# Row sums over a 64 MB stream: one load into the first buffer, with a 1 KB scratch read issued ahead of it

## The chip, the cores and the metric

The kernel runs on one core of a Trainium2 chip. The metric is the device time of one execution in microseconds (us). Some executions of a program can fall in a slower state; all runs of the two kernels, and of every variant that was timed in rounds (before and variant in turn), were in the fast state, with a granted clock of 1.0.

## The reference

```python
def setup_inputs():
    batch, seq, dim = 32, 512, 1024
    return {"x": np.random.randn(batch, seq, dim).astype(np.float32)}

def reference(x):
    return np.sum(x, axis=-1).astype(np.float32)
```

There are 16,384 rows of 1,024 float32, 67.11 MB in. 64 KB come out.

## The kernel before

The rows are cut into two blocks of 112 and 16 rows per partition. A buffer `xt` takes 16 rows on each of 128 partitions, which is 64 KB a partition and 8.39 MB in all, and there are three such buffers. DVE (VectorE) sums 16 rows with one reduction. ACT (ScalarE) helps only near the end. All loads are issued by SP (SyncE). The first buffer is filled by two loads: one row per partition, then the other 15.

```python
    xpool = ctx.enter_context(tc.tile_pool(name="x", bufs=3))
    ...
        while c < whole:
            m = min(G, whole - c)                       # G = 16
            xt = xpool.tile([P, G * D], F32, tag="xt", name="xt")
            parts = (0, 1, m) if done + c == 0 else (0, m)
            for i, k in zip(parts, parts[1:]):
                nc.sync.dma_start(
                    out=xt[:, i * D : k * D], in_=x_b[:, (c + i) * D : (c + k) * D]
                )
            a = ACT_ROWS if done + c + m == full else 0
            rows_dve(xt, res, 0, m - a, c)
            rows_act(xt, res, m - a, a, c + m - a)
            c += m
    ... # the last 16 rows of each partition in six smaller loads, summed by DVE and ACT
```

After the program is built, the first `EARLY = 2` DMA instructions of SP are moved from the body into the entry block, ahead of the barrier with which the engines start:

```python
    loads = [i for i in code if i.engine == sp][:EARLY]
    for load in loads:
        assert load.opcode == "DMACopy" and not load.sync_info.on_wait
        code.remove(load)
    ...
    at = next(k for k, i in enumerate(code) if i.engine == sp and i.opcode == "Drain")
    code[at:at] = loads
```

## Time and profile before

| What | Before | Where it is read |
|---|---|---|
| time | 162.29 us (162.26 to 162.44, 3 runs) | times |
| span of the profiled run | 160.5 us | page |
| one 16-row reduction on DVE | 17.22 us | groups by form |
| one 8.39 MB buffer | every 19.35 us, 433.5 GB/s | starts of the reductions in the timeline |
| first reduction starts | 21.81 us | timeline |

The first fence has two lines of the groups kept apart by form: line, engine, operation, names, shapes and count; then busy us and mean ns; then the idle time before the group and what ended it. The second is from the waits: who waited for whom, us in total, times, longest.

```profile
line engine op names shapes xcount | busy us, mean ns | idle before us <-releasers
L41 DVE TENSOR_REDUCE res<-xt 128x16 f32<-128x16384 f32 x6 | 103.3, 17220 | 32.4 <-DMA xt<-in_x_dram 32.4
```

```profile
DVE res L41 <- DMA xt<-in_x_dram: 34.5, 7, 21.8
```

DVE always waits for DMA: 21.8 us for the first buffer, and about 2.1 us for each of the others, since a buffer takes 19.35 us to arrive and 17.22 us to sum. The timeline shows the pace (start, duration, then the instruction):

```profile
21.81 17.22 DVE L41 TENSOR_REDUCE res<-xt 128x16 f32<-128x16384 f32 x1 [21.81 <-DMA xt<-in_x_dram]
41.09 17.22 DVE L41 TENSOR_REDUCE res<-xt 128x16 f32<-128x16384 f32 x1 [2.06 <-DMA xt<-in_x_dram]
60.44 17.22 DVE L41 TENSOR_REDUCE res<-xt 128x16 f32<-128x16384 f32 x1 [2.13 <-DMA xt<-in_x_dram]
...
118.49 17.22 DVE L41 TENSOR_REDUCE res<-xt 128x16 f32<-128x16384 f32 x1 [2.13 <-DMA xt<-in_x_dram]
```

The Trainium skill, "DMA: Bandwidth & Descriptors", section "Where 436 GB/s comes from", gives 435.2 GB/s as the ceiling of the 16 SBUF ports that the DMA engines write through; the 433.5 GB/s here agree within 0.4%. (The same section says that for loads from HBM a lower limit of about 358 GB/s binds, though it also names a load measured at 425; here the measured pace lies above both.) By this ceiling the kernel has next to nothing to gain from the first buffer on. What is left is the start.

The start is best seen in two views. First, SP's line of the timeline: its first four loads, of which the first, row 0, is issued at 0.00 us.

```profile
0.00 2.28 SPq L79 DMA_DIRECT2D xt<-in_x_dram  x4
```

Then the view of busy time by stretches: the stretch, its length, the busy time of DVE, ACT and POOL, the clock, the DMA share (mean of 16 engines), and GB/s.

```profile
0.00:1.00 1.00, 0.00 (x0) 0.00 (x0) 0.20 (x4) 1.00 0.00 0
1.00:1.50 0.50, 0.00 (x0) 0.00 (x0) 0.00 (x0) 1.00 1.42 115
1.50:2.00 0.50, 0.00 (x0) 0.00 (x0) 0.00 (x0) 1.00 0.39 147
2.00:2.50 0.50, 0.00 (x0) 0.00 (x0) 0.00 (x0) 1.00 1.00 401
```

A packet is one contiguous piece that a DMA engine moves. This view books a packet, with all its bytes and all its time, in the stretch in which it begins; that is why a share can exceed 1. It also lets one count packets and find their mean duration. From 1.0 to 1.5 us, 115 GB/s for 0.5 us are 57 KB, so 14 packets of 4 KB began. Their time is 1.42 x 0.5 us x 16 engines = 11.4 us, so 0.81 us each. From 2.0 to 2.5 us there are 49 packets of 4 KB with 1.00 x 8 = 8 us, so 0.16 us each. **The first packet on an engine is slow, by about 0.6 us; those behind it are not.** The stored trace also has the start, duration and size of every single packet, though not its engine, and `prof` has no view that lists them. The text calls these the packet records; engines are told apart in them only by which packet begins as another ends.

### The profile page before, as it was taken

To read this page: it belongs to the slowest core of one execution; us is meant where nothing else is said; L and a number is where in the kernel's file an instruction comes from. 1 tells how busy PE (TensorE), PEld (TensorE's weight loads), DVE (VectorE), ACT (ScalarE), POOL (GpSimd) and SP (SyncE) were. 2 spreads that over 40 slices of the span, in tenths; PEclk is the share of its full clock that TensorE was granted. 3 is DMA by queue.
4 is the path that set the end of the run, shared out by engine and by line. 5 is a ranking of instruction groups with operands and counts; after the bars stand their busy time and mean duration, and the time that the engine had idled before them with its cause. 6 is when DMAs were issued, how large, how long until landed. Compare 5 with 4: busy or idle time off the path is not lost.

```text
span 160.5 us, 118 instructions
## 1 busy us (share of the span) xinstructions
DVE 122.7 (76%) x14; ACT 16.0 (10%) x29; POOL 0.2 (0%) x4
## 2 busy tenths in 40 slices
DVE  0000059997799959999499994999949998699992
ACT  0000000000000000000000000000000000692892
POOL 0000000000000000000000000000000000000000
DMA  9979996996996996996996996996997998999991
GB/s 376 490 306 429 490 523 261 523 523 261 523 523 261 523 523 261 523 523 261 523 523 261 523 506 278 523 506 278 523 474 310 523 425 359 392 425 425 419 401 46
DMA packets 2304, 67.18 MB, mean 418 GB/s; under 512 B 512, under 2 KB 640, under 8 KB 1024
## 3 DMA queue, kind: packets, MB, share of 16 engines
q1 hardware_dynamic: 2160, 67.12, 97.3%
q10 hardware_dynamic: 144, 0.06, 0.1%
HBM read 67.11 MB, written 0.07 MB: 418 GB/s over the span
## 4 chain that ended last, share of the span: by engine, by line
DMA 74%; DVE 22%; SPq 1%; issue 0%; DVEq 0%
DMA xt<-in_x_dram 74%; DVE res L41 21%; SPq L93 1%; DVE xt L57 1%; DVEq L57 0%; DVE part L57 0%; DVEq L114 0%
## 5 line engine op out<-in xcount | busy, mean ns | idle before, releaser
L41 DVE TENSOR_REDUCE res<-xt 128x16 f32<-128x16384 f32 (+4 forms) x10 | 121.8, 12203 | 34.5 <-DMA xt<-in_x_dram 34.5
L49 ACT ACT_TABLE_LOAD x1 | 1.3, 1283 | 137.9 <-DMA xt<-in_x_dram 137.9
L49 ACT ACTIVATE xt<-xt 128x1024 f32<-128x1024 f32 x14 | 14.6, 1042 | 3.7 <-DVE res L41 3.7
L49 ACT ACTIVATION_READ_ACCUMULATOR xt<-xt 128x1 f32 x14 | 2.6, 186 | 0.0
L57 DVE CUSTOM_DVE_ANT_0 xt<-xt 128x288 f32<-128x288 f32 x1 | 0.5, 459 | 0.9 <-DMA xt<-in_x_dram 0.9
L57 DVE CUSTOM_DVE_ANT_0 xt<-xt,part 128x224 f32<-128x224 f32 x1 | 0.5, 452 | 0.1
L151 POOL MEMSET const-uint8-127<- 128x1 uint8 x1 | 0.1, 102 | 0.0
L151 POOL MEMSET const-bfloat16-1.0<- 128x1 bf16 x1 | 0.1, 101 | 0.0
L151 POOL MEMSET const-float32-0.0<- 128x1 f32 x1 | 0.1, 98 | 0.2 <-issue 0.2
L151 POOL MEMSET const-float32-1.0<- 128x1 f32 x1 | 0.1, 98 | 0.0
L57 DVE DVE_READ_ACCUMULATOR2_ANT res<- 128x1 f32 x1 | 0.1, 84 | 0.0
L57 DVE DVE_READ_ACCUMULATOR2_ANT part<- 128x1 f32 x1 | 0.1, 83 | 0.0
## 6 DMA issues: line engine op xcount, KB each, us to landing
xt<-in_x_dram SPq DMA_DIRECT2D x1, 7680.0 KB, 21.3
xt<-in_x_dram SPq DMA_DIRECT2D x1, 4096.0 KB, 31.1
xt<-in_x_dram SPq DMA_DIRECT2D x1, 2048.0 KB, 35.7
xt<-in_x_dram SPq DMA_DIRECT2D x2, 512.0 KB, 21.1
xt<-in_x_dram SPq DMA_DIRECT2D x1, 1024.0 KB, 37.8
xt<-in_x_dram SPq DMA_DIRECT2D x1, 288.0 KB, 38.9
xt<-in_x_dram SPq DMA_DIRECT2D x1, 224.0 KB, 38.9
xt<-in_x_dram SPq DMA_DIRECT2D x6, 40.8
```

Source lines behind the costliest of these rows:

```text
L41: nc.vector.tensor_reduce(out=res[:, c : c + n], in_=xt[:, j * D : (j + n) * D].rearrange("p (j d) -> p j d", d=D), axis=X, op=ADD,)
L49: nc.scalar.activation(out=v, in_=v, func=COPY, accum_out=acc)
L57: nc.vector.tensor_tensor_reduce(out=xt[:, a:h], in0=xt[:, a:h], in1=xt[:, h:b], scale=1.0, scalar=first, op0=ADD, op1=ADD, accum_out=acc,)
L93: nc.sync.dma_start(out=xt[:, i * D : k * D], in_=x_b[:, (c + i) * D : (c + k) * D])
L151: nc = _bacc.Bacc("TRN2", target_bir_lowering=False, num_devices=1)
```

## The change

Its intent, as the name `warm` says: let a tiny read meet that slow first access, so that the first buffer can come in one load without the split. The scratch tile is never read.

```diff
+    warm = rpool.tile([16, 16], F32, name="warm")
...
-            parts = (0, 1, m) if done + c == 0 else (0, m)
-            for i, k in zip(parts, parts[1:]):
-                nc.sync.dma_start(
-                    out=xt[:, i * D : k * D], in_=x_b[:, (c + i) * D : (c + k) * D]
-                )
+            if done + c == 0:
+                nc.sync.dma_start(out=warm, in_=x_flat[0:16, 0:16])
+            nc.sync.dma_start(out=xt[:, 0 : m * D], in_=x_b[:, c * D : (c + m) * D])
```

The rest of the diff changes no instruction. `EARLY` is still 2, so the scratch read and the whole first load now stand ahead of the barrier.

More of the change, by code (lines that the diff above doesn't have):

```diff
@@ L118 @@
     sp = mybir.EngineType.SP
+    fn = tc.nc.m.functions[0]
     entry, body = None, None
-    for blk in tc.nc.m.functions[0].blocks:
+    for blk in fn.blocks:
         ops = [i for i in blk.instructions if i.engine == sp]
```

## The prediction

> **What bounds the kernel.** The input stream. In the timeline the 16-row reductions on DVE start at 21.81, 41.09, ..., 118.49 and 137.84 us, so one 8.39 MB buffer arrives every 19.35 us ((137.84 - 41.09) / 5), which is 433.5 GB/s. The Trainium skill (DMA: Bandwidth & Descriptors, "Where 436 GB/s comes from") puts the ceiling at 435.2 GB/s; the trace agrees within 0.4%. One reduction takes 17.22 us (groups by form), so DVE waits some 2.1 us for each buffer, always on DMA (waits: 34.5 us in 7 waits, 21.8 of them the first load). The queue never runs dry: the load issues (DMA queue's waits) come when a reduction frees a buffer, e.g. at 39.06 us, while a whole further load is still queued. So the end is: start of the stream + 67.11 MB at 433.5 GB/s (154.8 us) + a tail. The last load lands at 157.1; 157.1 - 154.8 = 2.3 us is all that the start costs, and the change touches only this.
>
> **The start before, from the packet records.** Row 0's load is issued at 0.00 us, the load of rows 1 to 15 at 0.43, the next two at 1.26 and 1.64. First packets start at 1.00 us. They take 0.60 to 1.01 us on 14 of the 16 DMA engines, where later 4 KB packets take 0.159; on the other two the first packet starts only at 1.81 us. So every engine is slow once, [...]and ends its first packet 1.75 to 2.18 us in. Then come seven 4 KB packets (about 0.157 us each) and eight of 60 KB (2.27): 19.26 us per engine. The first buffer is full at 21.39 us.
>
> **What the change does.** Instruction order: two DMAs are still moved ahead of the start barrier, now the 1 KB scratch read and the whole first load; the other 14 DMAs, their order, the buffers and all compute are the same. One extra wait on a semaphore in the issue of the tail loads asks for something long done. Nobody reads the scratch tile.
> Removed: 128 packets of 4 KB. Added: 16 packets of 64 B. The first load becomes eight 64 KB packets per engine, at 2.418 us 19.34 us.
> If the slow first access is paid once per engine by whatever comes first, the scratch read pays it between 1.0 and about 1.65 to 2.05 us (estimate: row 0's first packet less its 0.16 us of transfer plus a little), and the big load, issued at 0.43 and ready about 1.0 us later (the same lag as row 0's), follows without a gap: full at about 21.3 us, 0.1 us earlier. If the big load has to pay a second latency behind it, it is 0.4 to 0.6 us later. If the 64 B return sooner than 0.6 us, up to 0.3 us earlier. Any of these passes one to one to the end.
>
> **Predicted.** 162.3 us, range 161.8 to 162.8; faster by over 2% 0.005, within 2% 0.985, slower by over 2% 0.01. A 2% change (3.2 us) is more than the whole 2.3 us of start.
>
> **What would show it.** Reductions still 19.35 us apart and 17.22 us long; the first begins at 21.7 us (21.4 to 22.3), and the end shifts by as much as it does. First big packets start at 1.5 to 2.1 us and take about 2.42 us, not 3. Span 160.1 to 161.0.
>
> **What would make it wrong.** A scratch read far slower than row 0's first packets (its 16 rows lie within 64 KB of memory, so all engines may press on one place); a big load whose descriptors come later than row 0's; or a first-packet penalty that depends on size or address, so that it is paid by each of the big load's partitions.

## The result

| | before | changed |
|---|---|---|
| time, median | 162.37 us (162.26 to 162.58, 4 runs) | 162.83 us (162.75 to 162.92, 4 runs) |
| span of the profiled run | 160.5 us | 161.0 us |
| first reduction starts | 21.81 us | 22.20 us |

The ratio is 1.0027, 95% interval [1.001, 1.0044]: 0.46 us slower, small but outside noise. (Ratios here are the mean time of one kernel's fast runs over that of the other's of the same rounds, so not quite the ratio of the medians.)

The timeline after, the same reductions:

```profile
22.20 17.22 DVE L42 TENSOR_REDUCE res<-xt 128x16 f32<-128x16384 f32 x1 [22.20 <-DMA xt<-in_x_dram]
41.55 17.22 DVE L42 TENSOR_REDUCE res<-xt 128x16 f32<-128x16384 f32 x1 [2.13 <-DMA xt<-in_x_dram]
60.90 17.22 DVE L42 TENSOR_REDUCE res<-xt 128x16 f32<-128x16384 f32 x1 [2.13 <-DMA xt<-in_x_dram]
...
118.96 17.22 DVE L42 TENSOR_REDUCE res<-xt 128x16 f32<-128x16384 f32 x1 [2.13 <-DMA xt<-in_x_dram]
```

Every start is 0.39 to 0.47 us later than before, from the first to the last. From the second reduction on the pace is the same 19.35 us. So 0.39 us of the loss is there by 22.2 us, and it is carried to the end. The other 0.07 comes between the first two reductions, which were 19.28 us apart before and are 19.35 now; why was not traced. The waits say the same: 35.0 us in place of 34.5, the longest 22.2 in place of 21.8.

```profile
DVE res L42 <- DMA xt<-in_x_dram: 35.0, 7, 22.2
```

The SP issues after, from the timeline, and the scratch read's line of the DMA issues (KB each, us from issue to landing):

```profile
0.00 0.38 SPq L79 DMA_DIRECT2D warm<-in_x_dram  x1
0.44 1.62 SPq L80 DMA_DIRECT2D xt<-in_x_dram  x3
```

```profile
warm<-in_x_dram SPq DMA_DIRECT2D x1, 1.0 KB, 1.5
```

The big load is issued at 0.44 us, where row 0 was issued at 0.00. The scratch read has landed by 1.5 us. Then the stretches after:

```profile
1.00:1.50 0.50, 0.00 (x0) 0.00 (x0) 0.00 (x0) 1.00 1.61 526
1.50:2.00 0.50, 0.00 (x0) 0.00 (x0) 0.00 (x0) 1.00 4.65 1573
...
4.50:5.00 0.50, 0.00 (x0) 0.00 (x0) 0.00 (x0) 1.00 4.54 1966
```

From 1.5 to 2.0 us 12 packets of 64 KB begin (1573 GB/s x 0.5 us = 786 KB), with 4.65 x 8 = 37.2 us: 3.10 us each. From 4.5 to 5.0 us, the second packet on each engine, there are 15 with 36.3 us: 2.42 us each. **The big load pays the slow first packet in full (0.68 us), although the scratch read has been through every engine just before.** In the packet records the 16 scratch packets begin at 0.99 to 1.18 us and last 8 ns each. Their landings, 16 of them, come from 1.30 to 1.45 us, so 8 ns is not the whole way of the data; but no scratch packet is recorded as slow, as row 0's first packets were.

### The profile page after: what moved, and what is told of

Read it like the earlier page. It is cut to its first block, busy times and chain, and to the rows that moved or that the text cites. A ratio compares the mean times of both kernels' runs of the same rounds, so it can differ in the third digit from the quotient of the medians.

```text
span 161.0 us, 117 instructions
## 1 busy us (share of the span) xinstructions
DVE 122.7 (76%) x14; ACT 16.1 (10%) x29; POOL 0.2 (0%) x4
## 4 chain that ended last, share of the span: by engine, by line
DMA 74%; DVE 22%; SPq 1%; issue 0%; DVEq 0%
DMA xt<-in_x_dram 74%; DVE res L42 21%; SPq L92 1%; DVE xt L58 1%; DVEq L58 0%; DVE part L58 0%; DVEq L113 0%
```

## The experiments

Theory A: the scratch read absorbs nothing. It takes the first issue slot of SP, about 0.43 us, and the bulk load behind it starts that much later and pays its slow first packet anyway. The rivals are told in the expectations. Eleven kernels were run, all with right results. Two of them (one buffer; the bursts) were slow on purpose, and had one look each, so their state is not known; only packet times within the one run are compared there.

Those timed in rounds are summed up in this table, worked out from the issues, packet records and reductions of the profiled runs; times are medians. "First packets" are the first 16 in time of the first load with a whole buffer or most of it (in the two rows with *, of row 0's load): first and last start, and mean duration. With packets as short as 4 KB a few of these 16 are an engine's second. A 64 KB packet takes 2.42 us later on, one of 63 KB (quarter row) 2.38.

```
kernel        bulk load   first packets     mean    first       minus    time    ratio to before
              issued, us  start, us         us      reduction   issue    us      [95%]
before         0.00*       1.00 to 1.80*    0.73*    21.81      21.81    162.33
no_warm        0.00        0.99 to 1.86     3.07     21.85      21.85    162.46  1.0002 [0.9990, 1.0015]
swapped        0.00        1.00 to 1.48     3.17     21.99      21.99    162.52  1.0006 [0.9994, 1.0019]
warm_act       0.00        1.00 to 1.56     3.14     21.74      21.74    162.37  0.9998 [0.9984, 1.0012]
changed        0.44        1.47 to 1.76     3.12     22.20      21.76    162.83  1.0027 [1.0010, 1.0044]
same_addr      0.43        1.47 to 2.38     2.99     22.19      21.76    162.96  1.0036 [1.0020, 1.0051]
warm4k         0.43        1.49 to 2.33     3.10     22.37      21.95    162.96  1.0035 [1.0022, 1.0049]
row0_warm      0.44*       1.47 to 1.75*    0.47*    22.53      22.09    162.87  1.0028 [1.0015, 1.0042]
late_load      0.79        1.76 to 2.26     3.19     22.64      21.85    163.12  1.0044 [1.0028, 1.0059]
two_warms      0.88        1.92 to 2.66     3.07     22.80      21.92    163.38  1.0062 [1.0049, 1.0075]
quarter_row    0.41**      1.48 to 2.53     3.02     22.43      22.02    162.68  1.0017 [1.0005, 1.0030]
* row 0's load, packets of 4 KB, later ones 0.159 us    ** the second load
```

The ratio is to the kernel before of the same rounds, whose median was 162.37 us for the changed kernel, 162.45 for warm_act and quarter_row, and 162.33 for the others.

The column to look at is "minus issue". Whatever stands ahead of the bulk load, the first reduction starts 21.7 to 22.1 us after that load is issued.

**no_warm: without the scratch read** (and with `EARLY = 1`, so that the later loads stay where they were).

```diff
-            if done + c == 0:
-                nc.sync.dma_start(out=warm, in_=x_flat[0:16, 0:16])
```

> The change without its scratch read: one load of 8 MB fills the first buffer and is the first DMA issued. Theory A (the scratch read absorbs nothing; it only takes the first issue slot of about 0.43 us, and the load behind it still pays the slow first packet): first big packets start at about 1.0 us instead of 1.47 to 1.76, take 2.9 to 3.4 us, first reduction at about 21.8 us, time equal to the kernel before within 0.1 us, about 0.4 us under the changed kernel. Rival B (a 64 KB first packet is dearer than a 4 KB one, so the split of row 0 was what helped): time stays 0.3 to 0.5 us above the kernel before.

Measured: 162.46 us (162.35 to 162.48, 5 runs), ratio 1.0002. The first reduction starts at 21.85 us:

```profile
21.85 17.22 DVE L42 TENSOR_REDUCE res<-xt 128x16 f32<-128x16384 f32 x1 [21.85 <-DMA xt<-in_x_dram]
```

As theory A says. One load of 8 MB is as good a start as row 0 and the rest, within the interval (-0.1% to +0.15%); rival B falls. The medians differ by 0.13 us, which these rounds don't resolve.

**swapped: the same two DMAs in the other order.**

```diff
-            if done + c == 0:
-                nc.sync.dma_start(out=warm, in_=x_flat[0:16, 0:16])
             nc.sync.dma_start(out=xt[:, 0 : m * D], in_=x_b[:, c * D : (c + m) * D])
+            if done + c == 0:
+                nc.sync.dma_start(out=warm, in_=x_flat[0:16, 0:16])
```

> The changed kernel with its first two DMAs in the other order: the big load, then the scratch read. Theory A (only the issue slot ahead of the load costs): as without the scratch read, so equal to the kernel before within 0.1 us, first reduction about 21.8 us. Rival C (the extra DMA with its packets costs wherever it stands): stays near the changed kernel, 0.3 to 0.5 us above the kernel before.

Measured: 162.52 us, ratio 1.0006 [0.9994, 1.0019], first reduction at 21.99 us. The median is 0.19 us above the kernel before, more than the 0.1 expected, but the interval holds 1. The same instructions cost nothing that is clear of noise once the big load goes first, and all five runs (162.34 to 162.65) lie under all four of the changed kernel (162.75 to 162.92, in other rounds). It is the place of the read that costs; a cost of its presence of up to 0.3 us is not excluded by the interval, but warm_act shows no sign of one.

**row0_warm: the scratch read ahead of the kernel before.**

```diff
-EARLY = 2
+EARLY = 3
...
+            if done + c == 0:
+                nc.sync.dma_start(out=warm, in_=x_flat[0:16, 0:16])
             for i, k in zip(parts, parts[1:]):
```

> The kernel before with the scratch read put ahead of its row 0 load, all three issued ahead of the start barrier. Theory A: row 0's packets start near 1.45 us and the first of each engine still takes 0.6 to 1.0 us; time 0.35 to 0.5 us above the kernel before. The prediction's idea (the first access is paid once by whatever comes first): row 0's first packets take about 0.16 us and the time is within 0.1 us of the kernel before or under it. Rival B (the size of the first packets): equal to the kernel before within 0.15 us, since row 0 still comes in 4 KB packets.

Measured: 162.87 us (162.73 to 163.04), ratio 1.0028 [1.0015, 1.0042]: the loss of the change, without the change of the load. Row 0's packets start at 1.47 us, and early ones take up to 0.85 us; they are not at 0.16 us as the prediction's idea would have it. Nor do the first 16 take the 0.6 to 1.0 us expected of theory A: they average 0.47, and the slow part is spread over more packets (28 of the 128 took over 0.2 us, where 19 did before). Added up over the load, the time above 0.159 us a packet is 0.54 us an engine, against 0.60 in the kernel before, so hardly any of it was taken away. In the profiled run, with 163.03 us one of the slowest two of its five, the first reduction starts at 22.53 us, 22.09 after row 0's issue, the longest in the table.

**two_warms: the dose doubled.**

```diff
-EARLY = 2
+EARLY = 3
...
                 nc.sync.dma_start(out=warm, in_=x_flat[0:16, 0:16])
+                nc.sync.dma_start(out=warm2, in_=x_flat[0:16, 16:32])
```

> The changed kernel with a second scratch read behind the first (two DMAs ahead of the big load). Theory A: one more issue slot, so big packets start near 1.9 to 2.2 us, the first reduction at about 22.6 us, and the time is 0.35 to 0.5 us above the changed kernel, 0.8 to 0.9 above the kernel before. Rival B (size of the first packets): the time is that of the changed kernel within 0.15 us only if the second read's slot is hidden; it predicts no doubling.

Measured: 163.38 us, ratio 1.0062. One scratch read costs about 0.4 us over the kernel without it (162.46 to 162.83, in different rounds), two cost 0.92 (162.46 to 163.38, same rounds). The timeline shows why: each DMA takes SP about 0.43 us, and the big load is the third.

```profile
0.00 0.37 SPq L80 DMA_DIRECT2D warm<-in_x_dram  x1
...
0.42 0.41 SPq L81 DMA_DIRECT2D warm<-in_x_dram  x1
0.88 1.65 SPq L82 DMA_DIRECT2D xt<-in_x_dram  x3
```

The next question was why the scratch read does not absorb the slow first packet: too little time, wrong addresses, too few bytes, or because nothing ahead of the bulk can.

**late_load: more time between the two** (only the scratch read is moved ahead of the barrier).

```diff
-EARLY = 2
+EARLY = 1
```

> The changed kernel with only the scratch read ahead of the start barrier; the big load is issued behind it, at about 1.25 us instead of 0.44, so the scratch read has landed (1.5 us) well before the big load's packets start (about 2.2 us). Theory A (every start of the stream on idle DMA engines pays a slow first packet, whatever ran before): first big packets still take 2.9 to 3.4 us, first reduction at about 23.0 us, time 0.7 to 0.9 us above the changed kernel. The prediction's idea given more time (one early access pays for the engine): first big packets take about 2.45 us, first reduction at about 22.3 us, time within 0.2 us of the changed kernel.

The load was issued at 0.79 us, not at 1.25: behind one DMA in place of two, SP comes through the barrier earlier, so the sizes expected were too large. The scratch read had landed on every engine by 1.45 us, 0.3 us before the first big packet. Measured: first reduction 22.64 us, 163.12 us. The stretches:

```profile
1.50:2.00 0.50, 0.00 (x0) 0.00 (x0) 0.00 (x0) 1.00 5.23 1704
...
5.00:5.50 0.50, 0.00 (x0) 0.00 (x0) 0.00 (x0) 1.00 3.33 1442
```

13 packets with 41.8 us, so 3.22 us each; later 11 with 26.6 us, 2.42 each. More time, at least as little more as this, doesn't help. The load is issued 0.35 us later than in the changed kernel, and the time is 0.29 us longer by the medians (of different rounds).

**same_addr: the scratch read touches every place where the load begins.**

```diff
-    warm = rpool.tile([16, 16], F32, name="warm")
+    warm = rpool.tile([P, 16], F32, name="warm")
...
-                nc.sync.dma_start(out=warm, in_=x_flat[0:16, 0:16])
+                nc.sync.dma_start(out=warm, in_=x_b[:, 0:16])
```

> The changed kernel with the scratch read made of the first 64 bytes of each of the big load's 128 partitions, so every place where the load starts has been read. Theory A: first big packets still take 2.9 to 3.4 us; time that of the changed kernel, to 0.15 us more for the 8 small packets of each engine. Rival F (the slow first access belongs to the address): first big packets take about 2.45 us and the time falls by 0.4 us or more, to the kernel before or under it.

Measured: first packets 2.99 us on average, first reduction at 22.19 us as in the changed kernel, 162.96 us. Having been read at the address a moment ago is of no use; rival F falls. (The end is 0.13 us later than in the changed kernel by the medians, though the first reduction is not.)

**warm4k: 4 KB an engine in place of 64 bytes.**

```diff
-    warm = rpool.tile([16, 16], F32, name="warm")
+    warm = rpool.tile([16, D], F32, name="warm")
...
-                nc.sync.dma_start(out=warm, in_=x_flat[0:16, 0:16])
+                nc.sync.dma_start(out=warm, in_=x_flat[0:16, 0:D])
```

> The changed kernel with 4 KB instead of 64 bytes into each of the 16 scratch partitions, one packet of 4 KB on each DMA engine. Theory A with an overlap (the slow first packet is the fill of the stream; a first packet of some length carries it, and packets that queue up behind it while it is being paid do not pay again): the 4 KB packets take 0.6 to 1.0 us, the big ones behind them about 2.42 us, time 0.1 to 0.25 us above the kernel before. If the fill is paid by each DMA anew: big packets take 2.9 us or more and the time is that of the changed kernel or up to 0.3 us more.

Measured: 162.96 us, and the second of the two outcomes. The 4 KB packets take 0.16 to 0.21 us (0.17 on average) in the records, so they are not slow, though row 0's first packets, of the same size, are. The big packets behind them take 3.10 us. The overlap that was hoped for didn't happen.

**one_buffer: is it paid once, or at every start?** With one buffer each load waits for the reduction and starts on idle engines.

```diff
-    xpool = ctx.enter_context(tc.tile_pool(name="x", bufs=3))
+    xpool = ctx.enter_context(tc.tile_pool(name="x", bufs=1))
```

> The changed kernel with one input buffer instead of three, so each load is issued only when the reduction has freed the buffer and starts on idle DMA engines. Slow on purpose, about 300 us. Theory A (paid at every start from idle): the first 16 packets of every load take 2.9 to 3.4 us, the others 2.42. Rival D (a cold first access, once per run): only the first load's first packets are slow, the later loads' first packets take about 2.42. Rival E (the first packets are slow because the issues of the next loads fall into the same time): the same as D here, since nothing is issued behind the later loads.

Measured: 294.45 us, one look. The second load is issued at 39.56 us with nothing behind it; its stretches:

```profile
40.50:41.00 0.50, 0.00 (x0) 0.00 (x0) 0.00 (x0) 1.00 6.28 2097
...
43.50:44.00 0.50, 0.00 (x0) 0.00 (x0) 0.00 (x0) 1.00 4.54 1966
```

All 16 engines begin with packets of 3.14 us on average, and go on with 2.42. In the packet records it is the same for all seven loads: the first 16 packets average 2.98 to 3.21 us, the other 112 of each load 2.42. So it is not a cold first access of the run (D falls), and not the next issues that disturb it (E falls). Every bulk load that starts on idle engines (for six of the seven, idle for 18.5 us) pays about 0.6 to 0.8 us. In the kernel with three buffers the loads behind the first are queued, never start on idle engines, and never pay: in the changed kernel the first 16 packets of each of the other six whole-buffer loads average 2.42 to 2.45 us.

**bursts: how much must a read hold to meet it?** One buffer; in the reductions' 17 us scratch reads from the ACT queue on idle DMA engines.

```diff
+    bursts = [(1, 16), (1, 1024), (2, 1024), (4, 1024), (8, 1024), (1, 2048), ...]  # packets an engine, floats a packet
...
+                    nc.scalar.activation(out=probe[:, 0:w], in_=xt[:, 0:w], func=COPY)   # keeps them apart
+                    nc.scalar.dma_start(out=probe[0 : 16 * n, 0:w], in_=src[:, 0:w])
```

> A probe, slow on purpose (about 300 us), result still right: one input buffer, no scratch read at the start, and in the 17 us of each reduction, while the DMA engines are idle, three scratch reads from the ACT queue, each some 5 us behind the last, of 1, 2, 4 or 8 packets on each DMA engine and of 64 bytes to 64 KB a packet. It asks how much a read must hold before it meets the slow first packet. Theory A (the loss is the fill of the engine's pipeline: a read that ends before the engine has to wait for its own data returning does not show it): 1 packet of 64 B takes 8 ns and 1 of 4 KB about 0.166 us as in the earlier runs; somewhere between 1 and 8 packets of 4 KB a first packet of 0.6 to 1.0 us appears, and one packet of 64 KB takes 2.9 to 3.4 us; small packets with the same bytes in total behave alike (8 of 512 B, 4 KB an engine, take no extra time). Rival G (it depends on the number of packets and not on bytes): 8 packets of 512 B show the slow first packet and one packet of 64 KB does not.

Measured in the packet records (first 16 packets of a burst: shortest, mean, longest, ns):

```
8 packets of 512 B an engine   25 /  26 /  32      1 packet of 4 KB    156 / 202 / 239   again 156 / 190 / 229
8 packets of 1 KB              44 /  52 /  79      2 of 4 KB           156 / 165 / 227   again 156 / 164 / 201
8 packets of 2 KB              81 / 183 / 438      4 of 4 KB           156 / 200 / 341   again 380 / 536 / 729
                                                   8 of 4 KB           156 / 365 / 682   again 156 / 273 / 429
```

Bytes decide more than packets: of the four shapes with 8 packets an engine, which fill all 128 partitions, 512 B and 1 KB show nothing, while at 2 KB and 4 KB (16 and 32 KB an engine) first packets are drawn out. It is a gradual onset that scatters between two bursts of one shape, and not the sharp 0.6 to 1.0 us expected. Rival G falls on its first half. Nor is size the whole of it: 8 of 4 KB is row 0's shape, and met less here (365 and 273 ns on average) than row 0 did with the rest of the stream queued behind it (0.73 us). The single packets of 8 KB and more can't be used: they went into only 16 partitions, and one of 32 KB took 3.1 to 4.0 us where the 32 KB packets of the 128-partition load take 1.21 (8 KB: 0.31 to 0.47 against 0.31), so something else slowed them, which no run here tests. The shapes of 1, 2 and 4 packets also filled only 16, 32 and 64 partitions.

**warm_act: the read from another queue, at the same time** (with `EARLY = 1`; the lines left out move the read ahead of ACT's part of the start barrier).

```diff
-                nc.sync.dma_start(out=warm, in_=x_flat[0:16, 0:16])
+                nc.scalar.dma_start(out=warm, in_=x_flat[0:16, 0:16])
...
```

> The changed kernel with its scratch read issued from the ACT queue, ahead of the start barrier, at the same time as the big load from the SP queue; so it takes no issue slot ahead of the load. Theory A (the slot is the whole cost, the read absorbs nothing): as without the scratch read, 162.35 to 162.55 us, first big packets from about 1.0 us and 3.0 to 3.2 us long on average. If the read absorbs some of the slow first packet after all, and only its slot hid that: under 162.2 us, first big packets under 2.9 us on average.

Measured: 162.37 us, ratio 0.9998 [0.9984, 1.0012]. Without a slot on SP the read costs nothing. It brings nothing either, but that is no test of absorbing: ACT issued at 0.12 us, and on each engine its packet ran only at 4.0 to 4.5 us, behind the first big one. The Trainium skill, "DMA: Bandwidth & Descriptors", section "Issuing engines are not separate DMA queues", says that issuing from several engines saves only the sequencer's time; this run agrees: 162.37 us against 162.83 with the read issued by SP (in other rounds), about one issue slot less.

**quarter_row: how much of row 0 is needed.** The kernel before, with a first load of 1 KB a partition.

```diff
-            parts = (0, 1, m) if done + c == 0 else (0, m)
+            parts = (0, D // 4, m * D) if done + c == 0 else (0, m * D)   # in elements
...
```

> The kernel before with its first load cut from one row (8 packets of 4 KB on each DMA engine) to a quarter of a row (8 packets of 1 KB); the second load takes the rest. In the probe 8 packets of 1 KB met no slow first packet and 8 of 4 KB did. Theory A (a DMA ahead of the bulk hides its issue slot only if it holds enough to make the engines wait for data itself): the slow first packet moves to the second load, whose packets start near 1.45 us and take 2.8 us or more where 60 KB to 64 KB take 2.3 to 2.4; less the 8 KB already moved on each engine (0.3 us), the time is 0.1 to 0.3 us above the kernel before. Rival B2 (any real data first, in small packets, starts the stream as well as a row): equal to the kernel before within 0.1 us, second load's packets without a slow first one.

Measured: 162.68 us, ratio 1.0017 [1.0005, 1.003]: 0.23 us by the medians, inside theory A's 0.1 to 0.3. The 1 KB packets take 44 to 128 ns, and the second load's first packets 3.02 us, 0.64 more than the 2.38 of the later ones. The profiled run, with 162.97 us the slowest of its five, is 0.29 us above the median, so its first reduction (22.43 us) is later than in a usual run. The interval alone would hardly exclude rival B2's 0.1 us (0.06%); the slow packets of the second load do. A first load that is too short loses part of the slot, as a scratch read loses all of it. One whole row, 32 KB an engine, meets the slow start itself, and the load behind it doesn't: all of its packets took 2.27 to 2.30 us.

## Why the prediction was wrong

- **The bound and the reach of the change: right.** The stream sets the time at 19.35 us a buffer; the shift at the first reduction (0.39 us) is found at 118 us as 0.47. The 2% classes were right.
- **The big load's timing: right.** "Issued at 0.43 and ready about 1.0 us later": issued at 0.44, first packets at 1.47 us.
- **"If the slow first access is paid once per engine by whatever comes first, the scratch read pays it between 1.0 and about 1.65 to 2.05 us": this step failed.** The scratch packets took 8 ns in the records and had landed by 1.45 us. The big load then paid 0.51 to 0.98 us above 2.42, though "3" us was named as the sign of being wrong and 3.12 is what came. The prediction took the slow packet for a cost of first access that a packet of any size pays, though every first packet in its trace was of 4 KB. The runs showed it to be a cost of every bulk start from idle, in all seven loads of the one-buffer run (2.98 to 3.21 us in place of 2.42), which neither 64 bytes nor 4 KB an engine sent ahead take away.
- **The sum built on that step.** It put the first buffer at 0.1 us earlier. With the step mended, the load starts 0.44 us later and saves nothing, so +0.44 us; measured +0.46 by the medians, 0.39 at the first reduction of the profiled runs. The branch "if the big load has to pay a second latency behind it, it is 0.4 to 0.6 us later" was the true one; it was named and then given too little weight, and the range ended at 162.8, 0.03 us short of the result. It is also mis-worded: there is no second latency, only one, started later.
- **Evidence that was there.** In the kernel before, row 0's first packets ended between 1.75 and 2.18 us on every engine, and two engines began late, at about 1.8 us, with a packet of normal length. That fitted a start-up of the stream as well as a cold access, and nothing in a single start can tell these apart.

What stays open: what inside the DMA engines or the memory path makes a bulk start slow. The runs show when it is paid, and that it tends to grow with the bytes asked of each engine at once; a pipeline that must fill is an argument that fits, not a thing shown. No version was found that beats the kernel before: the variants with the bulk load first (no_warm, swapped, warm_act) are the same as it within their intervals.

## What to carry to other kernels

When a stream is bound by bandwidth, its first bulk load should be the first DMA issued; a DMA ahead of it that carries next to none of the stream delayed the whole kernel here by its issue slot (0.43 us). A tiny warm-up read is worth a trial only if a second start of the same stream, on engines gone idle again, is fast: if that start is slow too, there is nothing to warm. A small useful load in front did no harm here when it was a whole row (32 KB an engine), and some when it was a quarter; that what counts is whether it keeps the engines busy until the next load's packets come is a reading that fits, not one that was tested.

## What the Trainium skill lacked or had wrong

- "DMA: Bandwidth & Descriptors", "Latency and other measured facts", gives about 0.6 us to the first byte for DMAs issued by SP or ACT. The trace agrees if one counts from the end of the issue to the start of the first packet: scratch read issued from 0.00 to 0.38 us, first packet at 0.99. The section gives no length for the issue itself, which comes on top: 0.36 to 0.43 us here for the DMAs ahead of the barrier (SP could issue its next DMA after 0.43). That accounts for the cost of this change (0.46 us).
- The same section has the HBM access latency as 0.2 us on average and 2 us at high load. No page says that a bulk load starting on idle engines loses some 0.6 to 0.8 us in the first packet of each engine, each time anew (64 KB packets: 3.0 to 3.2 us on average, then 2.42), while reads of 64 B to 8 KB an engine, in packets of up to 4 KB, show next to none of it.
